# Output projection of a hybrid mixer layer: one level of Strassen's product in place of the plain product

## Chip, cores, metric

One core of one Trainium2 chip. The metric is the device time of one execution in microseconds (us). The kernel before: 795.58 us, the median of three runs (793.99 to 796.27).

## What is computed

One layer in float32 over 512 tokens of width 2048. The normalised input is projected to six groups of 1024 channels; two mixers (attention with eight heads, and a gated linear recurrence with eight channel groups) make sixteen blocks of 128 channels; the output projection is a product of 512 x 2048 by 2048 x 2048, and the input is added to it.

```python
proj = jnp.einsum('bsd,de->bse', xn, w_in[l])
...
y_sb = y_sb * jax.nn.silu(g_sb)
...
y_lru = y_lru * jax.nn.silu(g_lru)
y = jnp.concatenate([y_sb, y_lru], axis=-1)
h = h + jnp.einsum('bse,ed->bsd', y, w_out[l])
```

## The kernel before, in words

Every large product is made from float32r parts: an operand is split into a high part (a cast on ACT) and a low part (a subtraction on DVE), and three matmuls of 128 x 128 by 128 x 512 stand for one.

The input projection runs in twelve groups (`in_group`, L232): for p in 0..3 the groups qk, xg and vg, each over sixteen blocks of 128 input channels, with four PSUM banks. After qk the attention weights of two heads are made (`attention_weights`), after xg two groups of the recurrence (`lru`), and after vg the values, gates and gated outputs of two heads (`finish_vg`, L478, and `attention_values`). The sixteen pairs of split input tiles, `xh` and `xl`, fill the pool `xy` until the last matmul of the last vg group has read them. So finished gated blocks go to DRAM (`finish_y`, L336, `y_dram`): fourteen of the sixteen, all but those of heads 6 and 7.

The output projection (L531 to L564) first brings those fourteen blocks back (`split_y`, L499: a load `yr`, a cast `yh` on ACT, a subtraction `yl` on DVE, into the places of `xh` and `xl`). Then for each of four groups of 512 output columns it loads w_out in eight pieces of 512 KB (`load_w`, tiles `or`), splits each (`split_w`, L228 and L229, tiles `ho` and `lo`) and runs, for four blocks of 128 tokens, three matmuls for each of sixteen input blocks (L555 to L557, banks `ob`): 4 x 16 x 4 x 3 = 768 matmuls of 512 columns. Its blocks are taken in an order that leaves those made last to the end:

```python
order = [0, 1, 8, 9, 2, 3, 10, 11, 4, 5, 12, 13, 14, 15, 6, 7]
```

At the end of a group the bank is added to the input `xr` (L563) and stored (L564). The last tile of all is held in two banks, so that its last 256 columns alone are added and stored after the last matmul.

Each engine runs its instructions in a fixed order that a scheduler wrote when the program was built. Loads and stores are issued by SP, the `xr` loads by ACT; an issue that must wait holds back all that its engine issues after it. The transfers of SP and ACT take eight semaphores in turn (DMAHW0 to DMAHW7), and a transfer waits until the one before it on its semaphore has landed.

## Time and profile before

| | before |
|---|---|
| time, median of 3 runs | 795.58 us (793.99 to 796.27) |
| span of the profiled execution, first to last instruction | 794.3 us |
| PE busy | 788.0 us, 99% |
| DVE, ACT, POOL busy | 453.7, 413.2, 3.6 us |
| HBM read, written | 80.26 MB, 7.86 MB |
| chain that ended last | PE 99%, DMA 1% |

The page gives the profiled execution's span; what lies around it is not in the trace, and the span is 1.3 us under the median of the timed runs. Busy time of an engine is the sum of its instructions' times; matmuls overlap, so their pace is the distance from start to start in the timeline. The DMA share is how busy the sixteen DMA engines were on average, and can exceed 1.

### The profile page before, as it was taken

Reading aid. Unit: us, or ns where it says so; the run is one execution under the profiler, and the core shown is the slowest. Engines: PE = TensorE matmul, PEld = TensorE weight load, DVE = VectorE, ACT = ScalarE, POOL = GpSimd, SP = SyncE. Lnnn points to the kernel's source line nnn. Section 1 sums busy time; section 2 is a strip of 40 time slices with the busy share of each in tenths; the row PEclk is TensorE's granted clock in tenths of the full one; section 3 lists DMA queues with packets and bytes.
Section 4 is the critical chain, followed back from the end, with each engine's and each line's share of the span. In section 5 each row is a group of like instructions: output and inputs, shape, how many; then the busy total and the mean of one; then the engine's idle time right before and its main releaser. Section 6 shows DMA issues by size and latency. Waiting matters only on the chain.

```text
span 794.3 us, 10792 instructions
## 1 busy us (share of the span) xinstructions
PE 788.0 (99%) x3991; PEld 670.3 (84%) x3991; DVE 453.7 (57%) x806; ACT 413.2 (52%) x820; POOL 3.6 (0%) x23
## 2 busy tenths in 40 slices
PE   8999999999999999999999999999999999999998
PEld 7888889888888998888889988888998888888886
DVE  3554587783446897534487783446897933242422
ACT  4934668662346967324568672345977632221220
POOL 0000000000000000000000000000000000000000
PEclk9999999999999999999999999999999999999999
DMA  9522222323232222423222324332123757263511
GB/s 286 191 90 85 80 81 87 100 93 123 91 106 81 63 91 92 140 81 106 80 79 87 100 69 135 103 95 91 54 94 122 235 185 213 88 204 106 159 54 53
DMA packets 76968, 88.82 MB, mean 112 GB/s; under 512 B 5026, under 2 KB 61172, under 8 KB 76916
## 3 DMA queue, kind: packets, MB, share of 16 engines
q1 hardware_dynamic: 74468, 83.82, 32.9%
q10 hardware_dynamic: 2448, 4.33, 2.0%
q8 instruction: 31, 0.51, 0.3%
q14 instruction: 21, 0.17, 0.1%
HBM read 80.26 MB, written 7.86 MB: 111 GB/s over the span
## 4 chain that ended last, share of the span: by engine, by line
PE 99%; DMA 1%; SPq 0%; DVE 0%; issue 0%; DVEq 0%
PE ob L556 7%; PE ob L555 7%; PE ob L557 7%; PE z L355 4%; PE qk0b L279 2%; PE qk0b L280 2%; PE qk0b L281 2%; PE xg1b L281 2%; PE xg2b L281 2%; PE xg3b L281 2%; PE xg0b L280 2%; PE xg0b L281 2%; PE xg0b L279 2%; PE xg3b L280 2%; PE xg1b L279 2%; PE xg3b L279 2%
## 5 line engine op out<-in xcount | busy, mean ns | idle before, releaser
L556 PE MATMUL ob<-lo,yh 128*128 128x512 f32 (+1 forms) x256 | 97.8, 383 | 0.0
L557 PE MATMUL ob<-ho,yl 128*128 128x512 f32 (+1 forms) x256 | 96.6, 382 | 0.0
L228 ACT CAST ho<-or 128x512 fp32r<-128x512 f32 x64 | 38.9, 621 | 108.4 <-PE ob L557 77.3
L229 DVE TENSOR_TENSOR lo<-or,ho 128x512 fp32r<-128x512 f32 x64 | 43.3, 690 | 90.8 <-ACT ho L228 90.6
L555 PE MATMUL ob<-ho,yh 128*128 128x512 f32 (+1 forms) x256 | 95.1, 383 | 0.0
L557 PEld LDWEIGHTS ob<-ho,yl 128*128 128x128 f32 x256 | 48.1, 188 | 9.5
L555 PEld LDWEIGHTS ob<-ho,yh 128*128 128x128 f32 x256 | 48.0, 188 | 9.5
L556 PEld LDWEIGHTS ob<-lo,yh 128*128 128x128 f32 x256 | 48.1, 188 | 9.2
L280 PE MATMUL qk0b<-xl,hqk 128*128 128x512 f32 x64 | 27.1, 424 | 0.0
L367 ACT ACTIVATE sp<-z 128x128 f32<-128x128 f32 (+3 forms) x32 | 13.9, 434 | 25.1 <-PE z L355 24.9
L281 PE MATMUL qk0b<-xh,lqk 128*128 128x512 f32 x64 | 25.9, 405 | 0.0
L280 PE MATMUL xg0b<-xl,hxg 128*128 128x512 f32 x64 | 25.2, 393 | 0.0
L279 PE MATMUL xg1b<-xh,hxg 128*128 128x512 f32 x64 | 25.1, 392 | 0.0
L279 PE MATMUL xg2b<-xh,hxg 128*128 128x512 f32 x64 | 25.1, 392 | 0.0
L279 PE MATMUL xg3b<-xh,hxg 128*128 128x512 f32 x64 | 25.1, 392 | 0.0
L279 PE MATMUL xg0b<-xh,hxg 128*128 128x512 f32 x64 | 25.1, 392 | 0.0
L280 PE MATMUL xg1b<-xl,hxg 128*128 128x512 f32 x64 | 25.1, 392 | 0.0
L280 PE MATMUL xg2b<-xl,hxg 128*128 128x512 f32 x64 | 25.1, 392 | 0.0
L280 PE MATMUL xg3b<-xl,hxg 128*128 128x512 f32 x64 | 25.1, 392 | 0.0
L281 PE MATMUL qk1b<-xh,lqk 128*128 128x512 f32 x64 | 25.0, 391 | 0.0
L279 PE MATMUL qk3b<-xh,hqk 128*128 128x512 f32 x64 | 24.9, 390 | 0.0
L279 PE MATMUL qk2b<-xh,hqk 128*128 128x512 f32 x64 | 24.9, 390 | 0.0
(438 smaller groups left out, 2243.6 us busy)
## 6 DMA issues: line engine op xcount, KB each, us to landing
or<-in_w_out_dram SPq DMA_DIRECT2D x32, 512.0 KB, 3.8
qk0r<-in_w_in_dram SPq DMA_DIRECT2D x16, 256.0 KB, 4.8
xg0r<-in_w_in_dram SPq DMA_DIRECT2D x16, 256.0 KB, 2.9
vg0r<-in_w_in_dram SPq DMA_DIRECT2D x16, 256.0 KB, 3.1
qk1r<-in_w_in_dram SPq DMA_DIRECT2D x16, 256.0 KB, 3.0
xg1r<-in_w_in_dram SPq DMA_DIRECT2D x16, 256.0 KB, 2.9
vg1r<-in_w_in_dram SPq DMA_DIRECT2D x16, 256.0 KB, 3.0
qk2r<-in_w_in_dram SPq DMA_DIRECT2D x16, 256.0 KB, 3.0
```

What stands on the lines that cost most here:

```text
L228: nc.scalar.copy(h, raw[:, j, :])
L229: nc.vector.tensor_tensor(out=l, in0=raw[:, j, :], in1=h.bitcast(F32), op=ALU.subtract)
L279: nc.tensor.matmul(banks[b], lhsT=wh[:, cs], rhs=xh[kt], start=st, stop=False)
L280: nc.tensor.matmul(banks[b], lhsT=wh[:, cs], rhs=xl[kt], start=False, stop=False)
L281: nc.tensor.matmul(banks[b], lhsT=wl[:, cs], rhs=xh[kt], start=False, stop=sp)
L355: nc.tensor.matmul(o, lhsT=lhsT, rhs=rhs, start=start, stop=stop, skip_group_check=True)
L367: nc.scalar.activation(e, z, AF.Abs)
L555: nc.tensor.matmul(bank, lhsT=yh[kt][:, ts], rhs=wh[:, os], start=st, stop=False)
L556: nc.tensor.matmul(bank, lhsT=yh[kt][:, ts], rhs=wl[:, os], start=False, stop=False)
L557: nc.tensor.matmul(bank, lhsT=yl[kt][:, ts], rhs=wh[:, os], start=False, stop=sp)
```

## The change

The product is cut in halves along tokens, input blocks and output columns, and seven products of half size, with sums of their operands, take the place of eight. A half-size product (`product`, with its number i) has two halves m of 512 output columns, four pieces a of the input blocks, two blocks u of 128 tokens, two blocks j, and three matmuls: 96 matmuls of 512 columns, so 672 in all. For each (m, a) the weights, a tile of 128 x 1024, are split anew (`woh` on ACT, `wol` on DVE), and for each a the half of the gated blocks (`sh`, `sl`).

- Weight sums are not made by an engine: the tiles `c1` (eight of 512 KB) are loaded once, and after a product has split one, POOL issues a DMA that adds another quarter of w_out onto it (`add_c`). There are 32 such transfers, beside 24 plain loads (`c1`, `c2`, and `c3` into the places of `c2`).
- The four sums of gated blocks are made on DVE in pieces (16 additions of 512 columns).
- Results are combined on DVE: 48 additions and subtractions of 512 columns, 16 of them with an input tile loaded by ACT, and four copies on ACT (`e1`).
- Buffers are reused: when the last vg group has read the pools `xy`, `qk`, `raw` and `wsp`, their space goes to `c1`, `ya` (the gated blocks), and the split tiles; `c2`, `s7`, `s3` and the result tiles take the place of the mixer's pools. All blocks but those of heads 6 and 7 go through DRAM, as before for fourteen of sixteen; heads 6 and 7 are written into `ya` directly.
- The last tile is no longer kept in two banks.

```diff
-    xy_pool = ctx.enter_context(tc.tile_pool(name="xy", bufs=32))
...
+    xy_pool = proj.enter_context(tc.tile_pool(name="xy", bufs=32, side="right"))
...
-    split_y(order)
...
-    for n in range(4):
...
-            raw = load_w(w_out_v[:, k0:k0 + KC, ns], f"or{n}_{c}")
...
+    proj.close()
+    NA = 4
+    c1_pool = first.enter_context(tc.tile_pool(name="c1", bufs=8, side="right", reuse_waits="tile"))
+    a_pool = first.enter_context(tc.tile_pool(name="ya", bufs=4, side="right", reuse_waits="tile"))
+    wo_pool = first.enter_context(tc.tile_pool(name="wo", bufs=3, side="right", reuse_waits="tile"))
...
+    def load_c(pool, tag, s, h, m, a, name):
+        t = pool.tile([P, 2, 512], F32, tag=tag, name=name)
+        nc.sync.dma_start(t, w_out_a[s, :, a, :, h, m, :])
+        return t
+    def add_c(t, s, h, m, a):
+        nc.gpsimd.dma_start(t, w_out_a[s, :, a, :, h, m, :], accum_op=ALU.add)
...
+    for a in range(NA):
+        for m in range(2):
+            c1[m, a] = load_c(c1_pool, "c1", 0, 0, m, a, f"c1_{m}_{a}")
+        if a < NA - 1:
+            for b in range(2):
+                nc.sync.dma_start(ya[a][:, b], y_dram_a[:, a, b])
+    nc.sync.dma_start(ya[3][:, 1], y_dram_a[:, 3, 1])
+    late[6], late[7] = ya[3][:, 0, 0, :], ya[3][:, 0, 1, :]
+    finish_vg(3, banks, wts)
...
+    def product(i, pool, tag, src, w, after=None):
...
+                nc.scalar.copy(wh, w[m, a])
+                nc.vector.tensor_tensor(out=wl, in0=w[m, a], in1=wh.bitcast(F32), op=ALU.subtract)
+                if after is not None:
+                    after(m, a)
+                for u in range(2):
+                    us = slice(u * P, (u + 1) * P)
+                    for j in range(2):
...
+                        nc.tensor.matmul(out[m, u], lhsT=sh[:, j, us], rhs=wh[:, j, :], start=st, stop=False)
+                        nc.tensor.matmul(out[m, u], lhsT=sh[:, j, us], rhs=wl[:, j, :], start=False, stop=False)
+                        nc.tensor.matmul(out[m, u], lhsT=sl[:, j, us], rhs=wh[:, j, :], start=False, stop=sp)
...
+    p1 = product(1, ps_mm, "mm", a11, c1, add_to(c1, 0, 1))
+    c2 = {(m, a): load_c(c2_pool, "c2", 1, 1, m, a, f"c2_{m}_{a}") for m in range(2) for a in range(NA)}
...
+    p3 = product(3, ps_o, "o", s3, c2, add_to(c2, 0, 1))
...
+    p5 = product(5, ps_mm, "mm", s5, c1, add_to(c1, 1, 1))
...
+    p7 = product(7, ps_o, "o", s7, c2)
+    c3 = {(m, a): load_c(c2_pool, "c2", 1, 0, m, a, f"c3_{m}_{a}") for m in range(2) for a in range(NA)}
...
+    p2 = product(2, ps_mm, "mm", a12, c3)
...
+    p6 = product(6, ps_o, "o", s6, c1, add_to(c1, 1, 0))
...
+    p4 = product(4, ps_mm, "mm", a22, c1)
+    for k in MU:
+        tt(r21[k], p4[k], r21[k])
+        store(r21[k], 1, 0, *k)
```

The scheduler's orders differ at two places that matter here. The first is SP's queue around the end of the last vg group. Before, its transfers there are w_out pieces (`or`) and single gated blocks (`yr`), each free to go when its own small buffer is:

```order
L217 DMA or0_3_6279<-in_w_out_dram 128x2x512 [waits DMAHW4_49,DMAHW3_49,DVE_49]
L217 DMA or0_4_6313<-in_w_out_dram 128x2x512 [waits DMAHW5_49,DVE_49]
L503 DMA yr0_6080<-y_dram_133 128x512 [waits Pool_49]
L503 DMA yr1_6086<-y_dram_133 128x512 [waits Pool_49]
L503 DMA yr8_6092<-y_dram_133 128x512
L217 DMA or0_5_6347<-in_w_out_dram 128x2x512 [waits DMAHW6_49,DVE_49]
L503 DMA yr9_6098<-y_dram_133 128x512 [waits DMAHW7_49,DMAHW3_49,DVE_49]
L503 DMA yr2_6104<-y_dram_133 128x512 [waits DMAHW4_49,DMAHW0_49,DVE_49]
L503 DMA yr3_6110<-y_dram_133 128x512 [waits DMAHW5_49,DMAHW1_49,DVE_49]
```

None of these rows waits for PE: the gated blocks come back one by one between pieces of w_out, in the order in which the product takes them.

Now SP's rows in the same stretch, from the load behind `c1_0_0` on, are these:

```order
L547 DMA c1_1_0_6048<-in_w_out_dram 128x2x512 [waits DMAHW7_49]
L560 DMA ya0_6042<-y_dram_133 128x2x512 [waits DMAHW0_49,PE_49]
L560 DMA ya0_6042<-y_dram_133 128x2x512 [waits DMAHW1_49]
L547 DMA c1_0_1_6052<-in_w_out_dram 128x2x512 [waits DMAHW2_49]
L547 DMA c1_1_1_6054<-in_w_out_dram 128x2x512 [waits DMAHW3_49]
L560 DMA ya1_6043<-y_dram_133 128x2x512 [waits DMAHW4_49]
L560 DMA ya1_6043<-y_dram_133 128x2x512 [waits DMAHW5_49]
L547 DMA c1_0_2_6058<-in_w_out_dram 128x2x512 [waits DMAHW6_49]
L547 DMA c1_1_2_6060<-in_w_out_dram 128x2x512 [waits DMAHW7_49]
L560 DMA ya2_6044<-y_dram_133 128x2x512 [waits DMAHW0_49]
L560 DMA ya2_6044<-y_dram_133 128x2x512 [waits DMAHW1_49]
```

The first `ya0` row has a new wait, for PE: it is for the last vg matmuls, which read the space that `ya0` takes. The loads of `c1` behind it, which before (as `or`) were free to go, now stand behind that wait too. Counted from the first `ya0` row, the two rows of `ya2` are the ninth and the tenth transfer. SP goes straight on with:

```order
L547 DMA c1_0_3_6064<-in_w_out_dram 128x2x512 [waits DMAHW2_49]
L547 DMA c1_1_3_6066<-in_w_out_dram 128x2x512 [waits DMAHW3_49]
L345 DMA y_dram_133<-yl7_5635 128x512 [waits DMAHW4_49,DVE_49]
L561 DMA ya3_6045<-y_dram_133 128x2x512 [waits DMAHW4_49,DMAHW1_49]
L547 DMA c2_0_0_6296<-in_w_out_dram 128x2x512 [waits DMAHW2_49,PE_49,Activation_49]
```

The load of `ya3` now stands behind the store of the last recurrent block (`yl7`), which waits for DVE, and `c2` stands behind `ya3`.

The second place is ACT within the first product. The rows named `r12`, `r22` and `r11` are loads of the input for the residual, which ACT issues; they stand between the casts that the matmuls need (`oh1_a` of the gated piece a, `woh1_ma` of the weight piece m, a):

```order
L576 CAST oh1_1_6163<-ya1_6043 128x512 [waits DMAHW5_49,DMAHW4_49]
L594 CAST woh1_02_6188<-c1_0_2_6058 128x1024 [waits DMAHW6_49]
L616 DMA r12_00_6500<-in_x_dram 128x512
L616 DMA r12_01_6504<-in_x_dram 128x512 [waits DVE_49,Pool_49]
L616 DMA r12_10_6508<-in_x_dram 128x512 [waits DMAHW7_49,Pool_49]
L616 DMA r12_11_6512<-in_x_dram 128x512 [waits DMAHW0_49]
L576 CAST oh1_2_6184<-ya2_6044 128x512 [waits DMAHW1_49,PE_49]
L616 DMA r22_00_6672<-in_x_dram 128x512
L616 DMA r22_01_6676<-in_x_dram 128x512 [waits DMAHW2_49]
L616 DMA r22_10_6680<-in_x_dram 128x512 [waits DMAHW3_49]
L594 CAST woh1_03_6209<-c1_0_3_6064 128x1024 [waits PE_49]
L594 CAST woh1_10_6228<-c1_1_0_6048 128x1024 [waits PE_49,Activation_49]
```

Here two loads (`r22_01`, `r22_10`) wait on semaphores DMAHW2 and DMAHW3, on which SP's `c1_0_3` and `c1_1_3` were issued, the two transfers behind `ya2`. The casts below them, `woh1_03` and `woh1_10`, were not behind any load before. On PE the first product runs pieces a = 0, 1, 2 of m = 0, then a = 0, 1, 2 of m = 1, and piece 3 of both at the end.

## Rows read from the trace of the kernel before

**Rows 1.** The page: span, busy time of each engine, chain that ended last

```profile
span 794.3 us, 10792 instructions
...
PE 788.0 (99%) x3991; PEld 670.3 (84%) x3991; DVE 453.7 (57%) x806; ACT 413.2 (52%) x820; POOL 3.6 (0%) x23
...
PE 99%; DMA 1%; SPq 0%; DVE 0%; issue 0%; DVEq 0%
```

**Rows 2.** Stretches of the output projection: busy us, clock, DMA share, GB/s

```profile
core 0: us, PE busy (x) PEld busy (x) DVE busy (x) ACT busy (x) POOL busy (x), PEclk, DMA share, GB/s
615.00:635.00 20.00, 20.00 (x93) 16.61 (x92) 19.32 (x33) 14.15 (x26) 0.00 (x0) 1.00 0.72 232
635.00:655.00 20.00, 20.00 (x90) 16.57 (x89) 7.61 (x12) 6.55 (x11) 0.00 (x0) 1.00 0.56 189
```

**Rows 3.** Timeline, PE at the projection's start: start us, us, instruction

```profile
611.65 0.39 PE L281 MATMUL vg3b<-xh,lvg 128*128 128x512 f32 x1
...
615.38 0.48 PE L555 MATMUL ob<-ho,yh 128*128 128x512 f32 x1
615.70 0.39 PE L556 MATMUL ob<-lo,yh 128*128 128x512 f32 x1
615.93 0.39 PE L555 MATMUL ob<-ho,yh 128*128 128x512 f32 x1
```

**Rows 4.** Timeline, the program's end

```profile
790.29 0.28 PE L557 MATMUL tail_bank<-ho,yl 128*128 128x256 f32 x1
790.61 0.42 DVE L563 TENSOR_TENSOR xr<-tail_bank,xr 128x256 f32<-128x256 f32 x1 [0.29 <-PE tail_bank L557]
```

**Rows 5.** Three stretches in which the DMA engines were full

```profile
6.00:16.00 10.00, 9.02 (x32) 6.98 (x31) 5.93 (x10) 4.22 (x7) 0.00 (x0) 1.00 1.07 350
626.00:628.00 2.00, 2.00 (x11) 1.65 (x10) 2.00 (x3) 1.21 (x3) 0.00 (x0) 1.00 0.94 344
632.00:634.00 2.00, 2.00 (x10) 1.65 (x10) 2.00 (x4) 1.61 (x4) 0.00 (x0) 1.00 1.00 342
```

**Rows 6.** DMA issues: engine, count, KB each, median us to landing

```profile
or<-in_w_out_dram SPq DMA_DIRECT2D x32, 512.0 KB, 3.8
...
out_dram<-xr SPq DMA_DIRECT2D x15, 256.0 KB, 2.9
...
y_dram<-yl SPq DMA_DIRECT2D x8, 256.0 KB, 2.0
```

**Rows 7.** Timeline, ACT: instructions of 512 columns back to back

```profile
612.07 0.61 ACT L228 CAST ho<-or 128x512 fp32r<-128x512 f32 x1
612.58 0.63 ACT L314 ACTIVATE es<-vs 128x512 f32<-128x512 f32 x1
```

**Rows 8.** Timeline, DVE: additions of 512 columns back to back

```profile
606.88 0.68 DVE L317 SCALAR_TENSOR_TENSOR e1l<-gp1l,e1l 128x512 f32<-128x512 f32 x1
607.48 0.68 DVE L229 TENSOR_TENSOR lo<-or,ho 128x512 fp32r<-128x512 f32 x1
```

**Rows 9.** Timeline, SP: the store of the last recurrent block

```profile
630.05 0.32 SPq L338 DMA_DIRECT2D y_dram<-yl  x1
```

**Rows 10.** Timeline, PE early in the program, after its first waits

```profile
11.34 0.63 PE L280 MATMUL qk0b<-xl,hqk 128*128 128x512 f32 x1
11.77 0.63 PE L279 MATMUL qk0b<-xh,hqk 128*128 128x512 f32 x1
...
14.15 0.40 PE L280 MATMUL qk0b<-xl,hqk 128*128 128x512 f32 x1
14.39 0.40 PE L281 MATMUL qk0b<-xh,lqk 128*128 128x512 f32 x1
```

More of the change, by code (lines that the diff above doesn't have):

```diff
@@ L329, in silu_gate, with y_tile @@
         return g
-    ys = [None] * KT
     y_dram = dram.tile([KT, P, S], F32, name="y_dram")
-    SPILL = 14
+    late = {}
+    def y_tile(k, name):
+        if k in late:
+            return late[k]
+        return y_pool.tile([P, S], F32, tag="y", name=name)
     def finish_y(k, y):
-        if order.index(k) < SPILL:
+        if k not in late:
             nc.sync.dma_start(y_dram[k], y)
-        else:
-            ys[k] = y
     woff = [0, 512, 896, 1152]
@@ new lines, in hybrid_block_kernel @@
+    w_out_a = w_out[0].rearrange("(b a s p) (h m n) -> s p a b h m n", p=P, s=2, a=NA, h=2, n=512)
+    y_dram_a = y_dram.rearrange("(b a s) p t -> p a b s t", s=2, a=NA)
+    def load_c(pool, tag, s, h, m, a, name):
[4 more added lines that the diff above has]
+        nc.gpsimd.dma_start(t, w_out_a[s, :, a, :, h, m, :], accum_op=ALU.add)
+    ya = [a_pool.tile([P, 2, 2, 512], F32, tag="ya", name=f"ya{a}") for a in range(NA)]
@@ new lines, in hybrid_block_kernel, with split_s @@
+    sa_pool = ctx.enter_context(tc.tile_pool(name="sa", bufs=4, reuse_waits="tile"))
+    r_pool = ctx.enter_context(tc.tile_pool(name="res", bufs=4, reuse_waits="tile"))
+    ps_o = ctx.enter_context(tc.tile_pool(name="ps_o", bufs=4, space=bass.MemoryType.PSUM,
+                                          reuse_waits="tile"))
+    def split_s(i, a, src):
+        h = so_pool.tile([P, 2, 256], F32R, tag="sh", name=f"oh{i}_{a}")
+        l = so_pool.tile([P, 2, 256], F32R, tag="sl", name=f"ol{i}_{a}")
+        nc.scalar.copy(h, src)
+        nc.vector.tensor_tensor(out=l, in0=src, in1=h.bitcast(F32), op=ALU.subtract)
+        return h, l
@@ new lines, in hybrid_block_kernel, with tt, add_to @@
+    MU = [(m, u) for m in range(2) for u in range(2)]
+    def tt(out, in0, in1, op=ALU.add, eng=None):
+        (eng or nc.vector).tensor_tensor(out=out, in0=in0, in1=in1, op=op)
+    def add_to(tiles, s, h):
+        return lambda m, a: add_c(tiles[m, a], s, h, m, a)
+    a11 = [t[:, :, 0, 0:256] for t in ya]
+    a21 = [t[:, :, 0, 256:512] for t in ya]
+    a12 = [t[:, :, 1, 0:256] for t in ya]
+    a22 = [t[:, :, 1, 256:512] for t in ya]
+    p1 = product(1, ps_mm, "mm", a11, c1, add_to(c1, 0, 1))
@@ new lines, in hybrid_block_kernel @@
+    c2 = {(m, a): load_c(c2_pool, "c2", 1, 1, m, a, f"c2_{m}_{a}") for m in range(2) for a in range(NA)}
+    s7, s3 = [], []
+    for a in range(NA):
+        s7.append(sa_pool.tile([P, 2, 256], F32, tag="s7", name=f"s7_{a}"))
+        s3.append(sa_pool.tile([P, 2, 256], F32, tag="s3", name=f"s3_{a}"))
+        tt(s7[a], a11[a], a21[a], ALU.subtract)
+        tt(a21[a], a22[a], a21[a], ALU.subtract)
+        nc.vector.scalar_tensor_tensor(out=a11[a], in0=s7[a], scalar=-1.0, in1=a22[a], op0=ALU.mult,
+                                       op1=ALU.subtract)
+        tt(s3[a], a12[a], a11[a])
@@ new lines, in hybrid_block_kernel @@
+    s5, s6 = a21, a11
+    e1 = {}
+    for k in MU:
+        e1[k] = res("e1", f"e1_{k[0]}{k[1]}")
+        nc.scalar.copy(e1[k], p1[k])
+    p3 = product(3, ps_o, "o", s3, c2, add_to(c2, 0, 1))
+    r12 = {}
+    for k in MU:
+        r12[k] = load_res("r12", f"r12_{k[0]}{k[1]}", 0, 1, *k)
+        tt(r12[k], p3[k], r12[k])
+        tt(r12[k], r12[k], e1[k], ALU.subtract)
+    p5 = product(5, ps_mm, "mm", s5, c1, add_to(c1, 1, 1))
+    r22 = {}
+    for k in MU:
+        r22[k] = load_res("r22", f"r22_{k[0]}{k[1]}", 1, 1, *k)
+        tt(r12[k], r12[k], p5[k], ALU.subtract)
+        tt(r22[k], r22[k], p5[k], ALU.subtract)
@@ L568 @@
+    r21 = {}
+    for k in MU:
+        tt(r12[k], r12[k], p6[k], ALU.subtract)
+        store(r12[k], 0, 1, *k)
+        tt(f[k], p6[k], f[k])
+        tt(r22[k], r22[k], f[k], ALU.subtract)
+        store(r22[k], 1, 1, *k)
+        r21[k] = load_res("e1", f"r21_{k[0]}{k[1]}", 1, 0, *k)
+        tt(r21[k], r21[k], f[k])
+    p4 = product(4, ps_mm, "mm", a22, c1)
+    for k in MU:
+        tt(r21[k], p4[k], r21[k])
+        store(r21[k], 1, 0, *k)
+    first.close()
 _INS = ["x", "norm_gain", "w_in", "q_norm_gain", "k_norm_gain", "conv_w", "conv_b", "lru_w_a", "lru_b_a",
```

105 lines of the change are left out of this document (54 added, 51 removed).

## The prediction

> **What bounds the kernel now.** I read the page first: its line of busy times and the chain that ended last [rows 1]. PE is busy for 99% of the span and is 99% of the chain; DVE and ACT are far from it. So only PE's work and its waits count. Next come the stretches of the output projection [rows 2]: PE is busy for all of each 20 us at a granted clock of 1.00. The first stretch is special, though: there DVE is busy for 19.32 us of 20 and the DMA engines for 0.72 of the time, because fourteen gated blocks come back while the last two recurrent groups are still being finished. Covered work there is covered only barely. The timelines give the stage's edges: the last vg matmul starts at 611.65 and the first of the projection at 615.38 [rows 3], the last ends at 790.29 + 0.28 = 790.57 [rows 4]. Behind it stand one DVE addition and a store, up to 794.3.
>
> The 768 products take 790.57 - 615.38 = 175.2 us, 0.228 us each; two neighbours start 0.23 us apart (615.70 and 615.93 [rows 3]). A weight load takes 16.57 / 89 = 0.186 us [rows 2], less than that, so the pace is the matmul's own and another order of operands should not change it.
>
> **The change, part by part.** Everything is reckoned against the profiled execution (span 794.3 us; the median, 795.58, is 1.3 more).
>
> *A. Fewer matmuls.* 768 become 672, all of 512 columns with the same tile shape. 96 x 0.228 = **-21.9 us**. This is all of the gain.
>
> *B. The first product waits for gated blocks.* The first `ya0` load waits for the last vg matmul, whose space it takes, so SP starts at about 611.65 + 0.39 = 612.0 and all behind it stands there too. `ya2` is the tenth transfer from there: 10 x 0.524 = 5.24 MB. When the DMA engines are full they move 342, 344 and 350 GB/s [rows 5]; I take 343. A 512 KB load lands 3.8 us after its issue [rows 6], 1.5 of it transfer by that rate, so 2.3 us are latency. Alone, SP's queue lands `ya2` at 612.0 + 15.3 + 2.3 = 629.6, and its cast follows (ACT starts two of 512 columns 0.51 apart [rows 7], say 0.6 with the wait): 630.2. PE wants it after pieces 0 and 1, at 615.4 + 24 x 0.228 = 620.9. So at least **9.3 us** of wait. But before that, the first two POOL additions onto `c1` and three input loads on ACT (256 KB each, issued after the cast of piece 2's weights) are also let go. If they get an equal share ahead of `ya2`, they add 2 x 1.05 (an addition counted twice, see G) + 0.79 = 2.9 MB, 8.4 us: **17.7 us**. I take 17, near the upper end, since the stretch is short of transfer for its whole length and the additions are let go as early as the first split. The Trainium skill ("DMA: Bandwidth & Descriptors", section "Issuing engines are not separate DMA queues") says that transfers started by different engines run on the same sixteen DMA engines and interleave; by it B is the shared 17 rather than 9.3, and the sum +5.1 rather than -2.6. No row here shows such a stretch with POOL's transfers in it.
>
> *C. Loads in ACT's way.* `r22_01` and `r22_10` wait on the semaphores of `c1_0_3` and `c1_1_3`, the eleventh and twelfth transfers, 2 x 1.53 = 3.1 us after `ya2`, or 6.1 if the additions share. Behind them stand two casts of 1024 columns, twice 0.51 = 1.02 each, and on DVE the subtractions, twice the 0.60 between neighbours [rows 8], 1.20 each. Meanwhile PE has the 12 matmuls of piece 2 (2.7 us) and ACT's cast is already counted (0.6). Low: 3.1 + 2.04 + 1.2 - 2.7 - 0.6 = **3.0**; high: 6.1 + 2.04 + 2.4 - 2.7 - 0.6 = **7.2**. In keeping with B I take 6.5.
>
> *D. The last recurrent block.* Its store went out at 630.05 [rows 9], 2.0 us to landing [rows 6], and `ya3` then needs 3.8 as a load of 512 KB. PE wants piece 3 after 72 matmuls and the waits above, at 615.4 + 16.4 + 23.5 = 655. That is covered by 15 us. But `c2` stands behind `ya3` on SP, and the third product needs sums of all blocks: 4.2 MB of `c2` take 12.2 us at full rate, up to 24 beside eight additions, against 661 when that product starts. 0 to 3; I take 1.5.
>
> *E. The tail.* The last addition is of 512 columns instead of 256: DVE 0.68 [rows 8] against 0.42 [rows 4]; the store is twice as large. 0 to 1; 0.5.
>
> *F. A slower start after a wait.* Early in the program, matmuls started 0.43 us apart (11.34, 11.77) and three us later 0.24 (14.15, 14.39), with the granted clock shown as 1.00 all along [rows 10]. That is the pace of the lower level, 1.2 GHz, after PE had waited for its data. With waits of 23.5 us (B and C) some of the first product may run so. Lower end 0; upper end 20 matmuls x 0.20 = 4.0; I take 1.5.
>
> *G. What is at no cost.* Weights are split 56 times in tiles of 1024 columns: on DVE 8 x 1.20 a product, with 4 x 0.60 for the gated pieces and some 7 x 0.60 for results (48 in 7 products), 16.2 of 21.9 us; on ACT 8 x 1.02 + 4 x 0.51 = 10.2. PE's own 21.9 us a product covers that. The sixth product has 16 result additions, 21.6 us: just covered, 0 to 1, which I leave in E. POOL, at 3.6 us busy [rows 1], now issues 32 additions; an issue could take 175 / 32 = 5.5 us before POOL bounded the stage, and only additions stand behind one another there. *Transfer* in the stage: plain, 24 x 0.524 of weights + 3.67 of gated blocks + 4.19 of input + 4.19 of output and little else from before, 23.8 to 24.6 MB; 32 additions are 16.8 MB counted once. No row shows an addition by DMA. Lowest price: that of a load, 1 x; highest: a load, a read of the tile and a store of it, 3 x. I take 2 x, between them, as a transfer that reads two things and writes one: 24 + 33.6 = 57.6 MB, 168 us of the 178 from 612 to 790. Covered, but without room. By 1 x, B would lose 2 x 0.524 / 0.343 = 3.1 us and C some 1.5, and the sum below would be +0.5. The Trainium skill ("Collectives: The Full Stack", section "Part 3: Why 7× under link rate — side-by-side accounting") says that an add within the DMA needs two source reads and so runs at about half the rate of a copy; by it the sum stays at +5.1. No row here shows it.
>
> *Sum:* -21.9 + 17 + 6.5 + 1.5 + 0.5 + 1.5 = **+5.1**: 799.4 in the profile, **800.7** on the median. So the forecast is slower by about 0.6%, with the whole loss in the first product.
>
> **The rivals.**
> 1. *The waits are at their low ends* (additions cheap or late, ACT's loads free): B 9.3, C 3.0, the others 0: -21.9 + 12.3 = -9.6, **786.0**. For it: SP issues ahead of the additions, and the old stage leaves the DMA engines at 0.56 after 635 [rows 2]. Against: B's low end already has SP's queue alone at full rate. If DVE's old load (19.32 of 20 us [rows 2]) still stands between 615 and 635, it is not reached.
> 2. *The additions bound the stage.* They are the only work that can: 178 us x 343 GB/s = 61 MB, so from (61 - 24) / 16.8 = 2.2 x on (2.4 x with the forecast's own longer stage) PE waits for DMA in the later products too. At 3 x: 24 + 50.3 = 74.3 MB less the last 1.05 MB of output = 213.6 us, so the last piece is summed at 825.6; a cast 1.0, a subtraction 1.2, 12 matmuls 2.7, an addition 0.7 and a store of 2.9 [rows 6] end at 834.1, or **835** on the median. For it: 168 of 178 us are taken by the middle price. Against: each sum has one or two whole products of time.
> 3. *Gain and waits cancel*: B near 13, C near 5, others 3 give -0.9, **795**.
> 4. *The gain is not there*, because PE's pace falls with other operands: excluded by equal shapes and by the 0.186 us of a weight load under 0.228. No chance of its own.
>
> **How the numbers follow.** Forecast 0.40, rival 1 0.26, rival 2 0.20, rival 3 0.14. A measurement tells about 0.3%, 2.4 us, from no change. Faster 0.26, the same 0.14, slower 0.60. The range reaches from 783, 3 under rival 1, to 833, just short of rival 2's price for 3 x; what lies outside is some 0.08 below and 0.1 above. The cases on the slower side up to 2.4 x lie between 798 and 808.
>
> **What would show it.** Right: PE's first product shows two long waits, 9 to 18 us up to the cast of `ya2` and 3 to 7 behind ACT's `r22` loads, and afterwards six products of about 22 us with PE full. D is right if the third product starts without a wait of over 3 us. G is right if the additions land within some 10 us and the DMA share stays at about 0.9 without PE waiting. Wrong: waits on `c1` or `c2` additions in the middle products (rival 2), a first product of less than 34 us (rival 1), or a distance of matmuls other than 0.228 in products 5 to 4 of the program (rival 4).

## The result, and the profile after

The changed kernel takes 807.13 us (806.71 to 807.18), the kernel before 795.41 us beside it: a ratio of 1.0152 (1.0135 to 1.0168), 11.7 us slower. The profiled execution spans 805.4 us, 11.1 more than before's. One of the four runs of a later kernel (e13) was slow, 960.39 us at a granted clock of 0.751, and stays out of the time given for it.

The page of the changed kernel, against [rows 1]: the span, the busy engines, the two DMA queues that matter (packets, MB, share of 16 engines' span), the chain.

```profile
span 805.4 us, 10605 instructions
...
PE 776.2 (96%) x3847; PEld 652.7 (81%) x3847; DVE 513.9 (64%) x857; ACT 441.4 (55%) x828; POOL 42.3 (5%) x55
...
q1 hardware_dynamic: 72180, 79.75, 30.7%
q0 software_dynamic: 8704, 16.78, 11.5%
...
PE 89%; DMA 9%; SPq 1%; DVE 0%; ACTq 0%; issue 0%; ACT 0%; DVEq 0%
```

PE's busy time fell from 788.0 to 776.2 us, and DMA rose from 1% to 9% of the chain. The queue q0 is POOL's: the 32 additions. Their packets took 11.5% of 805.4 us, 92.6 us of all sixteen engines, for 16.78 MB, which is 181 GB/s; q1 (SP's) by the same working moved 323.

PE's timeline at the first matmuls of the first product and at each wait after them (start, us, instruction, idle time before it and what ended it), against [rows 3]:

```profile
617.75 0.79 PE L602 MATMUL p<-woh,oh 128*128 128x512 f32 x1 [3.68 <-ACT oh L576]
618.34 0.63 PE L603 MATMUL p<-wol,oh 128*128 128x512 f32 x1
618.77 0.63 PE L602 MATMUL p<-woh,oh 128*128 128x512 f32 x1
...
621.93 0.39 PE L604 MATMUL p<-woh,ol 128*128 128x512 f32 x1
627.28 0.80 PE L602 MATMUL p<-woh,oh 128*128 128x512 f32 x1 [4.97 <-ACT oh L576]
...
631.80 0.40 PE L604 MATMUL p<-woh,ol 128*128 128x512 f32 x1
637.18 0.80 PE L602 MATMUL p<-woh,oh 128*128 128x512 f32 x1 [4.99 <-ACT oh L576]
...
641.85 0.40 PE L604 MATMUL p<-woh,ol 128*128 128x512 f32 x1
646.61 1.22 PE L602 MATMUL p<-woh,oh 128*128 128x512 f32 x2 [4.37 <-ACT woh L594]
648.66 0.80 PE L603 MATMUL p<-wol,oh 128*128 128x512 f32 x1 [0.83 <-DVE wol L595]
...
651.81 0.41 PE L602 MATMUL p<-woh,oh 128*128 128x512 f32 x1
```

The last matmul of the mixer ends at about 614.07 (613.68, two of 128 columns). Then PE waits 3.68 us for the first piece of the gated blocks, 4.97 for the second, 4.99 for the third, and 4.37 and 0.83 us behind it for weights: 18.84 us. After the waits matmuls first start 0.43 us apart (618.34, 618.77), not 0.23.

Stretches of the changed kernel, columns as in [rows 2]:

```profile
620.00:625.00 5.00, 2.32 (x8) 1.52 (x6) 3.86 (x6) 0.63 (x1) 1.21 (x1) 0.84 1.04 294
625.00:630.00 5.00, 2.71 (x6) 2.15 (x7) 3.10 (x5) 0.62 (x1) 0.00 (x0) 0.50 1.10 280
635.00:640.00 5.00, 2.82 (x7) 2.24 (x8) 2.53 (x4) 0.62 (x1) 0.00 (x0) 0.50 1.08 332
640.00:645.00 5.00, 2.24 (x7) 1.42 (x5) 0.00 (x0) 0.44 (x1) 0.00 (x0) 0.84 0.69 215
645.00:650.00 5.00, 2.56 (x5) 1.65 (x6) 3.25 (x4) 2.60 (x3) 2.30 (x2) 0.50 0.63 186
680.00:700.00 20.00, 17.83 (x73) 12.92 (x72) 16.46 (x20) 9.71 (x12) 8.38 (x7) 1.00 1.12 218
```

Up to 640 the DMA engines are full (shares of 1.04 to 1.10) and PE is busy for about half; from 640 to 650 they are not (0.69 and 0.63): until 645.4 SP stands for a store, as shown below. The granted clock drops to 0.50, the lower level of 1.2 GHz, in stretches in which PE waits for about half of the time. From 680 on PE runs at 1.00 again but is not full: the third product has a wait of half a microsecond for DVE's split at nearly every piece, as in these lines of PE's timeline, until 690:

```profile
677.73 0.50 PE L603 MATMUL p<-wol,oh 128*128 128x512 f32 x1 [0.53 <-DVE wol L595]
...
681.78 0.50 PE L603 MATMUL p<-wol,oh 128*128 128x512 f32 x1 [0.53 <-DVE wol L595]
```

Behind that split is ACT's cast, and behind the cast a transfer, as two of these casts show; they start 4.0 us apart:

```profile
675.37 1.05 ACT L594 CAST woh<-c 128x1024 fp32r<-128x1024 f32 x1 [2.92 <-DMA c<-in_w_out_dram]
679.42 1.05 ACT L594 CAST woh<-c 128x1024 fp32r<-128x1024 f32 x1 [3.00 <-DMA c<-in_w_out_dram]
```

Two long pieces of the chain that ended last (start, us, what), and SP's issue of `c2`, all eight loads in one row:

```profile
623.65 21.79 DMA y_dram<-yl
...
662.53 24.79 DMA c<-in_w_out_dram
```

```profile
645.97 17.76 SPq L547 DMA_DIRECT2D c<-in_w_out_dram  x8
```

And ACT at the fourth wait: the issue of three input loads, which waits, and the cast behind it:

```profile
636.52 8.00 ACTq L616 DMA_DIRECT2D r<-in_x_dram  x3
...
644.56 1.04 ACT L594 CAST woh<-c 128x1024 fp32r<-128x1024 f32 x1 [7.44 <-DMA c<-in_w_out_dram]
```

ACT stood 8.00 us in those issues. The transfer that the cast's row names is `c1_1_3`, on whose semaphore the last of the three loads, `r22_10`, waits; the cast itself reads `c1_0_3`, which SP issued one transfer earlier.

The store of the last recurrent block, 2.0 us before [rows 6], took 21.79 us to land; SP stood for the last 15.6 us of it before it could load the block, and only then, from 645.97 to 663.73, issued `c2`; six of these eight issues waited, 13.7 us in all, for input loads of ACT on the same semaphores. One of these loads took 24.79 us and landed at 687.32. The issues of the two kinds of weight transfers (count, KB, median us to landing) show that they were no exceptions, against 3.8 us for `or` [rows 6]:

```profile
c<-in_w_out_dram POOLq DMA_DIRECT2D x32, 512.0 KB, 12.3
c<-in_w_out_dram SPq DMA_DIRECT2D x24, 512.0 KB, 9.8
```

The end, against [rows 4]: the last matmul, the addition of 512 columns behind it.

```profile
800.80 0.39 PE L604 MATMUL p<-woh,ol 128*128 128x512 f32 x1
...
801.23 0.69 DVE L626 TENSOR_TENSOR r<-p,r 128x512 f32<-128x512 f32 x1 [0.44 <-PE p L604]
```

To compare kernels I reckon what PE loses in a product: the distance from the end of the product before (for the first, of the mixer's last matmul) to the end of its own 96 matmuls, less 96 x 0.228. A wait before a product's first matmul thus counts as that product's; where neighbouring products overlap by a few matmuls it is good to some 0.5 us. The changed kernel loses 27.5 us in its first product (product 1), 6.9 in the second to run (product 3), and -0.1 in each of the other five, where the matmuls run at 0.228 us: 33.7 in all, with unrounded figures. Each ratio is against the kernel before as it ran beside that kernel (medians of 794.97 to 795.65 us).

| kernel | time | ratio to before (95%) | lost in the 1st, 2nd, 3rd, 4th product run |
|---|---|---|---|
| before | 795.41 | | |
| changed | 807.13 | 1.0152 (1.0135 to 1.0168) | 27.5, 6.9, -0.1, -0.1 |
| e1 plain loads | 802.29 | 1.0088 (1.0063 to 1.0112) | 24.0, 4.4, -0.1, -0.1 |
| e2 input loads late | 812.57 | 1.0217 (1.0184 to 1.0251) | 19.4, 17.7, -0.1, -0.1 |
| e3 loads by need | 810.02 | 1.0180 (1.0157 to 1.0202) | 20.4, 15.8, -0.1, -0.1 |
| e4 last block direct | 808.26 | 1.0167 (1.0141 to 1.0193) | 30.8, 5.7, -0.1, -0.1 |
| e5 additions late | 794.18 | 0.9985 (0.9973 to 0.9998) | 21.1, -0.1, -0.1, -0.1 |
| e6 = e3 + e5 | 800.71 | 1.0076 (1.0059 to 1.0092) | 5.8, 17.2, 4.6, -0.1 |
| e7 = e6, input late | 803.08 | 1.0111 (1.0089 to 1.0133) | 9.7, -0.1, 11.6, 8.0 |
| e8 filled waits | 807.98 | 1.0163 (1.0146 to 1.0180) | 29.4, 3.8, -0.1, -0.1 |
| e9 = e7, other order of products | 794.30 | 0.9986 (0.9972 to 0.9999) | 8.0, 3.6, 1.5, 7.9 |
| e10 = e9, additions early | 801.26 | 1.0077 (1.0053 to 1.0102) | 17.2, 10.5, 0.7, -0.1 |
| e11 = e9, whole blocks | 800.97 | 1.0066 (1.0041 to 1.0092) | 13.6, 5.4, 8.3, -0.1 |
| e12 = e7, sums on POOL | 821.60 | 1.0333 (1.0318 to 1.0349) | 5.9, 4.8, 10.4, 13.9 |
| e13 = e5, input late | 806.10 | 1.0133 (1.0112 to 1.0153) | 13.3, 7.2, -0.1, 12.7 |
| e14 = e9, sums on POOL | 815.44 | 1.0259 (1.0236 to 1.0281) | 8.0, 6.1, 3.0, 7.0 |
| e15 = e9, r12 earlier | 793.79 | 0.9989 (0.9971 to 1.0007) | 7.7, 2.8, 9.6, -0.1 |
| e16 = e15 + e4 | 789.95 | 0.9941 (0.9917 to 0.9964) | 7.1, 1.8, 8.2, -0.1 |

### The profile page after: what moved, and what is told of

The parts are those of the page before. It is cut to its first block, busy times and chain, and to the rows that moved or that the text cites. A ratio compares the mean times of both kernels' runs of the same rounds, so it can differ in the third digit from the quotient of the medians.

```text
span 805.4 us, 10605 instructions
## 1 busy us (share of the span) xinstructions
PE 776.2 (96%) x3847; PEld 652.7 (81%) x3847; DVE 513.9 (64%) x857; ACT 441.4 (55%) x828; POOL 42.3 (5%) x55
## 3 DMA queue, kind: packets, MB, share of 16 engines
q0 software_dynamic: 8704, 16.78, 11.5%
## 4 chain that ended last, share of the span: by engine, by line
PE 89%; DMA 9%; SPq 1%; DVE 0%; ACTq 0%; issue 0%; ACT 0%; DVEq 0%
PE p L603 5%; PE p L604 5%; PE p L602 5%; PE z L360 4%; DMA c<-in_w_out_dram 3%; DMA y_dram<-yl 3%; PE qk0b L282 2%; PE qk0b L283 2%; PE qk0b L284 2%; PE xg0b L283 2%; PE xg3b L284 2%; PE xg2b L284 2%; PE xg1b L284 2%; PE xg0b L284 2%; PE xg2b L282 2%; PE xg3b L282 2%
## 5 line engine op out<-in xcount | busy, mean ns | idle before, releaser
L602 PE MATMUL p<-woh,oh 128*128 128x512 f32 x224 | 82.9, 409 | 18.8 <-ACT oh L576 13.6
L594 ACT CAST woh<-c 128x1024 fp32r<-128x1024 f32 x56 | 58.7, 1049 | 68.4 <-PE p L604 41.6
L595 DVE TENSOR_TENSOR wol<-c,woh 128x1024 fp32r<-128x1024 f32 x56 | 68.2, 1222 | 42.9 <-ACT woh L594 42.9
L603 PE MATMUL p<-wol,oh 128*128 128x512 f32 x224 | 91.0, 406 | 3.6 <-DVE wol L595 3.6
L604 PE MATMUL p<-woh,ol 128*128 128x512 f32 x224 | 88.7, 401 | 0.0
L602 PEld LDWEIGHTS p<-woh,oh 128*128 128x128 f32 x224 | 43.5, 196 | 31.3 <-ACT oh L576 14.7
L603 PEld LDWEIGHTS p<-wol,oh 128*128 128x128 f32 x224 | 43.9, 196 | 16.3 <-DVE wol L595 7.3
L551 POOL DMA_DIRECT2D c<-in_w_out_dram x32 | 38.7, 1211 | 262.0 <-DVE ql L471 138.7
L604 PEld LDWEIGHTS p<-woh,ol 128*128 128x128 f32 x224 | 43.7, 195 | 9.2 <-DVE ol L577 0.2
L372 ACT ACTIVATE sp<-z 128x128 f32<-128x128 f32 (+3 forms) x32 | 13.9, 434 | 25.1 <-PE z L360 24.9
L576 ACT CAST oh<-ya 128x512 fp32r<-128x512 f32 x20 | 12.4, 621 | 22.9 <-PE p L603 14.7
## 6 DMA issues: line engine op xcount, KB each, us to landing
c<-in_w_out_dram POOLq DMA_DIRECT2D x32, 512.0 KB, 12.3
```

What stands on the lines that cost most here:

```text
L372: nc.scalar.activation(e, z, AF.Abs)
L551: nc.gpsimd.dma_start(t, w_out_a[s, :, a, :, h, m, :], accum_op=ALU.add)
L576: nc.scalar.copy(h, src)
L594: nc.scalar.copy(wh, w[m, a])
L595: nc.vector.tensor_tensor(out=wl, in0=w[m, a], in1=wh.bitcast(F32), op=ALU.subtract)
L602: nc.tensor.matmul(out[m, u], lhsT=sh[:, j, us], rhs=wh[:, j, :], start=st, stop=False)
```

## The experiments

**What an addition costs (e1), and when it starts (e5).** In e1 only the addition was dropped from POOL's transfers; it leaves the sums out.

```diff
-        nc.gpsimd.dma_start(t, w_out_a[s, :, a, :, h, m, :], accum_op=ALU.add)
+        nc.gpsimd.dma_start(t, w_out_a[s, :, a, :, h, m, :])
```

> The 32 additions by DMA become plain loads of the same size on the same queue, with every engine's order unchanged; each sum of weights is thus replaced by the last quarter loaded, so the sums are left out. Theory (additions cost about two loads, and the loss lies in SP's and ACT's queues): the first product's third piece starts about 3 us sooner (two additions less one load's worth each), the casts behind the r22 loads 1 to 2 us, and of the 6.5 us lost in the third product about half is left; 798 to 801 us. Rival (the additions' transfer is what loses it all): B falls by 8, C and the third product's loss are gone, 785 to 790 us. If an addition cost no more than a load: 807 us.

Measured 802.29, 4.8 us less than the changed kernel, a little above the theory's range and far from the rival's. POOL's queue of e1, on the page:

```profile
q0 software_dynamic: 4608, 16.78, 7.8%
```

7.8% of 800.7 us is 62.5 us, against 92.6 as additions: 1.5 times as much, and nearly twice the packets (8704 against 4608). So an addition does cost more than a load, but taking that price away gives back only a seventh of the 33.7 us lost.

e5 leaves the price alone and moves the first eight additions behind the `c2` loads, by an addition of zero times a column of the `c2` tile.

```diff
-    p1 = product(1, ps_mm, "mm", a11, c1, add_to(c1, 0, 1))
+    p1 = product(1, ps_mm, "mm", a11, c1)
...
+            nc.gpsimd.tensor_scalar(out=zero, in0=c2[m, a][:, 0, 0:1], scalar1=0.0, scalar2=None, op0=ALU.mult)
+            nc.gpsimd.tensor_tensor(out=col, in0=col, in1=zero, op=ALU.add)
+            add_c(c1[m, a], 0, 1, m, a)
```

> The changed kernel, but each addition onto a c1 tile by the first product first waits on POOL for the c2 tile with the same numbers to land (POOL adds 0 times one of its columns to the tile). New theory (up to the third product's last weights the DMA engines are full, and what comes too early there takes the place of what is wanted; how the queues are ordered matters less): eight additions go from before 670 to after about 645; the third piece comes 4 to 6 us sooner, the third product's loss goes, and the fifth product waits 0 to 5 us for sums: 794 to 801 us. Rival (the bytes only move): the fifth product waits for as much as is won before it, 805 to 810 us.

Measured 794.18, 13 us less than the changed kernel, at the theory's lower end. The second product to run loses nothing, the first 6.4 us less, and the third, which reads those sums, does not wait. The additions then run with little beside them, in this stretch (columns as in [rows 2]):

```profile
670.00:700.00 30.00, 30.00 (x134) 24.82 (x134) 23.67 (x28) 15.34 (x18) 16.91 (x15) 1.00 1.13 207
```

207 GB/s at a share of 1.13: 0.524 MB in 2.53 us, against 1.53 at the 343 GB/s of [rows 5], 1.65 times. So it matters more when the additions start (13 us) than what each costs (4.8 us). Even so the store of the last recurrent block took 13.8 us in e5, without an addition under way, and `c2` was issued only from 641.53 on.

**The fourth wait (e2, e13).** e2 ties every input load to the end of the first product.

```diff
+        nc.scalar.copy(t[:, 0:1], p1[1, 1][:, 0:1])
         nc.scalar.dma_start(t, x2[ts, ns])
```

> Each load of the input on ACT now waits for the end of the first product, by a copy of one column on ACT into its tile; nothing else is changed in the program. Theory: the two casts of the fourth wait are free once the third piece is there, so the 4.4 + 0.8 us wait before 648.7 goes or shrinks to 1 us, and three loads less ahead of ya2 give 2 us more: 798 to 801 us. Rival (the fourth wait is DVE's and the weights', and the loads only stand beside it): 805 to 808 us, with the same wait at another instruction.

The fourth wait went, and the first product lost 8 us less, but the time rose to 812.57, outside both guesses. SP had issued `c2` from 640.30 to 653.37; the input loads followed on ACT from 657.45 on, and five of them stood there 15.71 us, with the cast of a `c2` tile behind them:

```profile
662.37 15.71 ACTq L617 DMA_DIRECT2D r<-in_x_dram  x5
...
678.18 1.04 ACT L594 CAST woh<-c 128x1024 fp32r<-128x1024 f32 x1 [14.79 <-DMA c<-in_w_out_dram]
```

The same standing as at the fourth wait thus came back in product 3, as PE's timeline shows:

```profile
679.28 1.22 PE L602 MATMUL p<-woh,oh 128*128 128x512 f32 x2 [11.97 <-ACT woh L594]
```

e13 does it from e5's side, with the loads on SP and gated on POOL behind `c2` and later products.

```diff
-        nc.scalar.dma_start(t, x2[ts, ns])
+        if gate is not None:
+            nc.gpsimd.tensor_copy(t[:, 0:1], gate)
+        nc.sync.dma_start(t, x2[ts, ns])
```

> As e5 (the changed kernel's own loads, first additions behind c2), with the loads of the input taken from ACT to SP, behind c2 and later, as in e7. Theory of term C (the 4.4 + 0.8 us wait in the first product is ACT's casts standing behind r22 loads): that wait goes, the first product loses 15 to 17 us instead of 21.3, the others 0 to 5: 788 to 794 us. Rival (that wait is for weights that come no sooner): the wait stays at 4 to 6 us, 793 to 797 us.

The wait behind the third piece fell from e5's 4.24 + 0.83 us to this one:

```profile
635.94 0.50 PE L603 MATMUL p<-wol,oh 128*128 128x512 f32 x1 [1.19 <-DVE wol L595]
```

The first product lost 7.8 us less than in e5. So term C is what it was said to be: ACT's casts standing behind its loads. But the time is 806.10, against both guesses: products 3 and 7 lose 20 us instead. There DVE stood for the late input loads, with the next split behind it, most of all here:

```profile
666.53 0.69 DVE L628 TENSOR_TENSOR r<-p,r 128x512 f32<-128x512 f32 x1 [6.61 <-DMA r<-in_x_dram]
```

**The order of loads (e3, e6, e7).** e3 loads first what the first product reads.

```diff
-            for b in range(2):
-                nc.sync.dma_start(ya[a][:, b], y_dram_a[:, a, b])
+            nc.sync.dma_start(ya[a][:, :, 0], y_dram_a[:, a, :, 0])
```

> The gated blocks are loaded by halves of the input blocks: first what the first product reads (four pieces of 512 and 256 KB, each behind its c1 piece of the first output half), then c1 of the second half and the other blocks; the scheduler then puts the r loads behind the casts too. Theory: before the third piece there are 6 transfers of 512 KB instead of 10, so it is there at about 623 to 628 instead of 637, and there is no wait behind r22: the first product ends 14 to 20 us sooner. The third product then starts at about 645 and waits for the late blocks and c2, which the same bytes bring no sooner than about 650 to 660: 8 to 12 us are given back. 790 to 800 us. Rival (the additions' bytes bound the stage as a whole): nothing is won, 804 to 808 us.

The third piece no longer waits long, and yet the whole loss stays, as the rival said, though the time is above the rival's too: 36 us, now nearly half of it in the second product, whose weights wait for late blocks and `c2`:

```profile
668.25 1.22 PE L605 MATMUL p<-woh,oh 128*128 128x512 f32 x2 [10.60 <-ACT woh L597]
```

e6 adds e5's late additions, e7 also the late input loads.

> The loads in the order of need (as in e3) and the first additions after c2 (as in e5). New theory: what the first and third products read is 11.5 MB, 34 us at full rate, there at about 648 if alone, against 36 us of loss with e3's order; the residual loads on ACT (3.1 MB, 9 us) still come early. First and third product lose 8 to 16 us together, the fifth 0 to 6: 783 to 794 us. Rival (the stage as a whole is bound by bytes): 804 to 810 us.

> As e6, and the loads of the input are issued by SP, each set only when it will be used: the first after c2 has landed, the second after the third product's results, the third after the fifth's. New theory: only what is wanted is under way up to about 650; first and third product lose 3 to 8 us together, the fifth 0 to 6: 777 to 787 us. Rival: as e6, the residual loads never having mattered, within 3 us of it.

e6 (800.71) falls between the guesses, and its first two products lose 23 us, more than forecast; e7 (803.08) is within the rival's 3 us of e6. In e7 the first and second product lose 9.6 us together, a little over the forecast, and the third and fourth 19.6: what was won early is given back later. e6 is slower than e5, though it loads in the order of need.

**The last block (e4).** It goes from its tile straight to its place.

```diff
-    nc.sync.dma_start(ya[3][:, 1], y_dram_a[:, 3, 1])
+    nc.sync.dma_start(ya[3][:, 1, 0], y_dram_a[:, 3, 1, 0])
+    nc.sync.dma_start(ya[3][:, 1, 1], late[15])
```

> The last recurrent block goes from its tile on chip to its place in one transfer, without a store to DRAM and a load behind it; all else stays. Theory: the third product's loss (6.5 us) is SP's queue standing until 645.5 for that store's landing, so c2 is issued from about 632 on and the loss falls to 0 to 2 us; the first product stays: 801 to 803 us. Rival (c2 is late because the additions take the transfer engines, whenever it is issued): the third product waits as before, 806 to 808 us.

808.26: no gain, just above the rival's range. SP's timeline shows it past the block at 632.22, and then standing for `c2` all the same:

```profile
631.63 0.59 SPq L564 DMA_DIRECT2D ya<-yl  x1
647.40 2.72 SPq L549 DMA_DIRECT2D c<-in_w_out_dram  x3
```

It stood 15.1 us there, for one of ACT's input loads to land, on whose semaphore the first `c2` load was to go. So `c2` was issued no sooner than in the changed kernel (647.40 against 645.97), and e4 can't tell what the wait for the store costs: one wait in the queue was taken out, and another stood behind it.

**The slow matmuls (e8).** 22 and 19 matmuls into a spare bank fill the waits behind the second and third piece.

```diff
+                if i == 1 and m == 0 and a < 3:
+                    for q in range((11, 11, 19)[a]):
+                        nc.tensor.matmul(spare, lhsT=sl[:, 1, 128:256], rhs=wh[:, 1, :], start=True, stop=True)
```

> The changed kernel with 41 more matmuls of 512 columns into an unused bank: 22 behind the second piece of the first product and 19 behind the third, where PE waited 5.0 and 4.4 us. Theory on the slower starts (0.43 us a matmul after a wait because PE had stood still): the pieces behind those two waits run at 0.23 from their first matmul, the third piece's gain of 2 us is lost again in the next wait and the one after the fourth wait is kept: 804 to 806 us. Rival (the slow matmuls wait for their operands): 0.43 us as before, 807 to 809 us.

PE's timeline: the third piece behind the fill, and the next wait, which the fill did not cover.

```profile
638.32 0.50 PE L604 MATMUL p<-woh,oh 128*128 128x512 f32 x1 [0.65 <-ACT oh L576]
638.65 0.40 PE L605 MATMUL p<-wol,oh 128*128 128x512 f32 x1
638.89 0.39 PE L604 MATMUL p<-woh,oh 128*128 128x512 f32 x1
...
650.88 0.79 PE L604 MATMUL p<-woh,oh 128*128 128x512 f32 x1 [5.25 <-ACT woh L596]
652.14 0.79 PE L605 MATMUL p<-wol,oh 128*128 128x512 f32 x1 [0.47 <-DVE wol L597]
652.73 0.63 PE L606 MATMUL p<-woh,ol 128*128 128x512 f32 x1
653.16 0.63 PE L604 MATMUL p<-woh,oh 128*128 128x512 f32 x1
```

Behind the fill matmuls start 0.24 us apart at once, behind the uncovered wait 0.43 again. So the slow starts come of PE's standing still, as the theory had it. The time did not move, though (807.98, in the rival's 807 to 809): only the last slow start counts, since the earlier ones end in the next wait for a transfer.

**Another order of products (e9, e10, e11).** The three products that read plain quarters of w_out come first, so that sums are wanted a product later.

```diff
+    p1 = product(1, ps_mm, "mm", a11, c1)
+    c3 = {(m, a): load_c(c2_pool, "c2", 1, 0, m, a, f"c3_{m}_{a}") for m in range(2) for a in range(NA)}
...
+    p2 = product(2, ps_o, "o", a12, c3)
...
+    c2 = {(m, a): load_c(c2_pool, "c2", 1, 1, m, a, f"c2_{m}_{a}") for m in range(2) for a in range(NA)}
...
+    p3 = product(3, ps_mm, "mm", s3, c2, add_to(c2, 0, 1))
+    p5 = product(5, ps_o, "o", s5, c1, add_to(c1, 1, 1))
+    p7 = product(7, ps_mm, "mm", s7, c2)
```

> As e7, but the products run in the order 1, 2, 3, 5, 7, 6, 4: the three that read plain quarters of w_out come first (the tiles of product 2 are loaded into the places that c2 takes next), so sums are wanted 22 us later; the first additions again wait for c2. New theory (what decides is which bytes are under way before they are wanted): the plain bytes of three products and the residuals are there by about 665 against 680, the sixteen additions of 2.54 us each by about 705 against 702 to 724. First product as in e7 (6 to 10 us lost), the others 0 to 4 together: 779 to 786 us. Rival (bytes of the whole stage bind, some 80 us of them before 700): 790 to 803 us.

> As e9 without the wait of the first additions: each starts as soon as the first product has split its tile. New theory: eight additions of 2.54 us take 20 us out of the stretch in which the blocks and the second product's weights come, so the first two products lose 12 to 20 us more than in e9, and nothing comes back later: 790 to 802 us. Rival (the order of the products alone is the gain): within 3 us of e9.

> As e9 with the gated blocks loaded as in the changed kernel (both input halves of a piece, and c1 of both output halves, piece by piece). New theory: the third piece of the first product waits for ten transfers again, so the first product loses 10 to 14 us more than in e9; the second has what it needs earlier and loses nothing: 786 to 796 us. Rival (order of loads within the first product evens out, as e3 against the changed kernel): within 3 us of e9.

e9 (794.30) is within the rival's range. e10 repeats e5 in this order: the additions let go early cost 7.0 us. The first product loses 9.2 us more than in e9 and the second 6.9, 16 together, as the theory had it; against "nothing comes back later", the fourth to run (product 5, the first that reads sums) loses 8.0 less. e11 (800.97) is outside both guesses, with 5.6 us more in the first product where 10 to 14 were expected; the order of loads, worth nothing in e3 while the additions came early, is worth 6.7 us in this order of products, where they don't.

**Sums on POOL (e12, e14).** A sum is a plain load and an addition by POOL; `so` has four buffers instead of six.

```diff
-        nc.gpsimd.dma_start(t, w_out_a[s, :, a, :, h, m, :], accum_op=ALU.add)
+        d = d_pool.tile([P, 2, 512], F32, tag="d", name=f"d{s}{h}_{m}_{a}")
+        nc.sync.dma_start(d, w_out_a[s, :, a, :, h, m, :])
+        nc.gpsimd.tensor_tensor(out=t, in0=t, in1=d, op=ALU.add)
```

> As e7 (original order of products), but a sum of weights is made by a plain load into a small tile, on SP's queue in its place in the order, and one addition of 128 x 1024 on POOL; four split tiles of gated blocks instead of six make the room. The same product is computed. New theory (with the order put right, the additions' transfer is what binds: 32 x 2.54 + 31 x 1.53 + 8.4 MB of residuals and results = 153 us of full DMA): plain loads bring it to 121 us, the first two products lose 6 to 10 us as in e7, the fifth and seventh 0 to 3 instead of 20: 779 to 786 us. Rival (POOL's addition is slower than the 2.7 us between two pieces, or holds DVE up): 795 us and more, with waits of ACT's casts on POOL.

> As e12 with e9's order of products. New theory: all plain bytes in the order of need, sums wanted 22 us later; first product 6 to 10 us, the second 3, the others 0 to 2: 779 to 785 us. Rival (POOL's additions): as in e12.

821.60 and 815.44, the slowest of all, as the rival said. Groups of e12 and e5 by line (count, busy us, mean ns of one):

```profile
L553 POOL TENSOR_TENSOR c<-c,d 128x1024 f32<-128x1024 f32 x32 | 86.2, 2698 | 41.3 <-DMA d<-in_w_out_dram 32.4 <-DVE wol L601 5.9 <-DVE r L634 3.0
```

```profile
L601 DVE TENSOR_TENSOR wol<-c,woh 128x1024 fp32r<-128x1024 f32 x39 | 83.2, 2152 | 5.4 <-ACT woh L600 5.4
```

```profile
L595 DVE TENSOR_TENSOR wol<-c,woh 128x1024 fp32r<-128x1024 f32 x50 | 60.8, 1223 | 28.9 <-ACT woh L594 27.1 <-DMA c<-in_w_out_dram 1.6
```

An addition on POOL takes 2.70 us on average (2.37 to 3.37), and DVE's split of the same size 2.15 (1.20 to 3.44) instead of 1.22: it is the short one with POOL idle and the long one beside an addition. The two engines hold each other up, and every piece of a product waits for that split. The DMA engines are relieved, but these runs can't say by how much the additions' price binds, since the new bound covers it.

**Two single waits (e15, e16).** In e9 DVE stood 4.38 us for an `r12` load, with the next split behind it:

```profile
695.74 0.69 DVE L631 TENSOR_TENSOR r<-p,r 128x512 f32<-128x512 f32 x1 [4.38 <-DMA r<-in_x_dram]
```

e15 lets those loads go with the second `c2` tile; e16 adds e4's edit.

```diff
-gate=c2[1, 3][:, 0, 0:1]
+gate=c2[0, 1][:, 0, 0:1]
```

> As e9, with the r12 loads let go once the second c2 tile has landed instead of the last. New theory (e9's 6 us at the start of the fifth product are DVE's r12 additions, which wait 4.4 and 0.8 us for those loads with the split of the next weights behind them): that wait goes, 787 to 790 us. Rival (the weights or sums are late there anyway, since the DMA engines are full): within 2 us of e9, with the wait at another instruction.

> As e15, and the last recurrent block goes to its place in one transfer on chip, as in e4. New theory (SP stood from 624 to 635.5 for that block, and the DMA engines were at 0.75 from 630 to 640): the second product's weights come some 4 us sooner, the first and second product lose 2 to 4 us less: 784 to 788 us. Rival: within 2 us of e15, as e4 against the changed kernel.

e15 (793.79) is within the rival's 2 us of e9: product 5 loses nothing any more, but product 3 loses 9.6 us instead of 1.5, with a wait of PE for ACT's cast of 4.37 us. e16 is faster: 789.95 us, 0.59% under before (0.36% to 0.83%) and the fastest of all, though not within the forecast: its first two products lose 1.6 us less than e15's, where 2 to 4 were expected. The same stretch in e15 and in e16 (columns as in [rows 2]):

```profile
630.00:640.00 10.00, 9.25 (x40) 7.00 (x39) 10.00 (x15) 5.03 (x8) 0.00 (x0) 1.00 0.74 228
```

```profile
630.00:640.00 10.00, 9.25 (x40) 7.00 (x39) 10.00 (x15) 5.39 (x8) 0.00 (x0) 1.00 1.04 374
```

In e15 the DMA engines are at 0.74 there, with SP standing for the last block's store until 634.88; in e16 SP goes straight on from the block (629.12) to the next eight weight loads (629.77 on), and the engines are full. In e4 another wait stood behind the one that the same edit took out.

## Why the prediction was wrong

The direction was right and the range held the time, but the forecast was 5.1 us and the spans differ by 11.1. The steps:

- **A, right.** Five of the seven products run at 0.228 us a matmul with no loss.
- **B, right in size and cause, by some luck in its parts.** The third piece's first matmul was put at 637.9 (620.9 + 17) and came at 637.18. That is 17.6 us behind PE's own start at 614.07 and 24 matmuls, near the shared end of the bounds. From SP's first `ya0` issue to the cast of `ya2`, 17.6 us were reckoned for SP's queue alone and 8.4 for the sharing, 26.0; measured are 26.0 (610.51 to 636.51). But in e13, with neither additions nor input loads let go early, the same stretch took 19.9 us (610.56 to 630.45): the queue alone was put 2.3 us short, and the sharing cost 6.1. That they share is also what a page states (the Trainium skill, "DMA: Bandwidth & Descriptors", section "Issuing engines are not separate DMA queues": transfers started by different engines run on the same engines and interleave); the trace agrees, with the casts of `c2` 4.0 us apart beside one addition each, where loads alone at full rate would come 1.53 apart.
- **C, a little small.** From 637.18 and 12 matmuls (2.7 us) to 646.61 are 6.7 us, and 0.83 for the split: 7.5, taken as 6.5 between 3.0 and 7.2, and just outside them. ACT's row of 8.00 us and e13 show the cause.
- **D failed.** "0 to 3; I take 1.5" was 6.9. It let the store go out at 630.05 and land in 2.0 us, the block load behind it in 3.8, so that `c2` would go from about 636 on and be there by about 660, against 661, in "up to 24" us beside eight additions. But the store took 21.79 us, `c2` was issued from 645.97 on, and its last load landed at 687.32, 41 us after the first was issued. In that time ran not only the first product's last five additions (issued from 647.17 to 658.07; the other three had gone by 633.14) but seven of the third product's own, each let go as soon as a `c2` tile is split (663.42 to 685.99), and these D left out. A load and an addition one after the other are 1.53 + 2.53 = 4.06 us, which is the distance of the casts, 4.0. e5 and e10 show what counts: with the first eight additions behind `c2` the loss is gone, and let go early in the other order of products they cost the second product 6.9 us. With plain loads in their place (e1) the second product still loses 4.4, so most of it is that these bytes are under way at all. What the late store costs by itself stays open, since e4 met another wait. D's own sign, no wait of over 3 us at the start of the third product, was met: the loss came as many short waits within it.
- **E, right**: from the last matmul's end to the span's, 3.7 us before (794.3 - 790.57), 4.2 after (805.4 - 801.19): 0.5.
- **F, small.** One slow start counts, 2.3 us (nine matmuls from 646.61 to 651.81: 5.2, less 9 x 0.228 and the wait of 0.83), taken as 1.5. Three more are hidden in the waits that follow them; e8 shows it for two.
- **G, the price was high, the conclusion too kind.** An addition cost 1.65 times a load by e5's stretch (1.5 by the packets' time in e1), against the 2 taken. The rule (the Trainium skill, "Collectives: The Full Stack", section "Part 3: Why 7× under link rate — side-by-side accounting") that an add within the DMA needs two source reads and so runs at about half the rate of a copy, which the page states for a ReduceScatter, has the right direction; here the measurement, 1.65, decides. By the 1.65 the stage's bytes fill 24 + 16.8 x 1.65 = 51.7 MB, 151 us of 178, which I called covered. As a sum over the stage that holds: e5 is 13 us faster with the same bytes. It does not hold for the first two products, where the DMA share is over 1.0 in four of the six stretches shown; over the whole program the additions land after 12.3 us at the median, where the sign said some 10.

The mixer's last matmul ended 1.3 us before the projection's start in the kernel before (614.07 against 615.38), which no term had; in the other kernels that keep the mixer it ended between 613.85 and 615.72, so this is scatter between executions. With it: -21.9 - 1.3 + 17.6 + 7.5 + 6.9 + 0.5 + 2.3 = 11.6, less some 0.4 in the other five products, of 11.1 measured. Of the 6 us by which the sum was off, D is 5.4. The slip in D that `ya3` is "covered by 15 us" (655 less 635.9 is 19) changes nothing.

Of the rivals, the second (the additions bound the stage) shares with the result only that PE waits for weights beside additions. Its condition, a price of 2.2 loads and a full stage, was not met: at 1.65 two products wait and five don't. What stays open: how much of e16's remaining loss (16.6 us over all seven products) is the additions' price; e12 and e14, meant to tell, met another bound.
